# Filter spectra by one radix-2 step, issued one group late, with filter inputs on GpSimd's queue and other buffers at the end of the start-up

## The chip, the cores and the metric

The kernel runs on one core of a Trainium2 chip. The metric is the device time of one execution in microseconds. Three timed runs of the kernel before took 2672.59, 2676.36 and 2677.06 us; their median, 2676.36 us, stands for it.

## The reference

Two layers of a diffusion backbone work on 256 latent tokens of width 2048, with 256 context tokens ahead of them: layer 0 is a Mamba-2 group beside a latent attention group, layer 1 a Hyena long convolution, and a SwiGLU feed-forward layer follows each. Every sub-layer is normed and modulated by shift, scale and gate that come from the conditioning vectors. The parts that this case touches are the modulation and the filters of layer 1:

```python
mod = (c_act @ mod_w[i] + mod_b[i])[:, None, :]
sh1, sc1, g1, sh2, sc2, g2 = jnp.split(mod, 6, axis=-1)
n_lat = modulate(rms_norm(x, norm_mix_w[i]), sh1, sc1)
...
hid = jnp.sin(fr * (emb @ fw1 + fb1))
for j in range(HY_INNER):
    hid = jnp.sin(fr * (hid @ fw_mid[j] + fb_mid[j]))
...
for i, gate in enumerate((x1, x2)):
    h_two = jnp.einsum('lf,fkd->lkd', hid, fw_out[:, i]) * window[:, None, :]
    k = jnp.concatenate([h_two[:, 0], zeros, jnp.flip(h_two[1:, 1], axis=0)])   # 512 x 2048
    k = k / jnp.sum(jnp.abs(k), axis=0, keepdims=True)
    kf = jnp.fft.rfft(k, axis=0)
    y = gate * (irfft(rfft(y, n=512) * kf)[:256] + fbias[i] * y)
```

The filters depend on no token, so the kernel computes their spectra at its start, beside the first modulation.

## The kernel before, in words

Products in fp32 are made of three: each operand is split into a high part (`fp32r`, on ScalarE, L347) and the remainder (on VectorE, L348), and `mm3` (L375 to L382) multiplies high by high (L380), low by high (L381) and high by low (L382).

The start-up (`startup`, from L1347) runs four generators by turns. A small function, `turn`, always advances the one that has done the least against its entry in `START_RATE`; `START_AT` gives the filters one turn of handicap. A scheduler then sets the order on each engine, while each queue (SP's for loads, ScalarE's for the stores of spectra) keeps the order in which its transfers were issued.

- `filters` (L703 to L787): loads of the small net's inputs (L707 to L712), three layers of matmul (L722) and sine (`sin_layer`, L691 to L702), then eight groups of 512 channels: four channel blocks by two filters. A group loads its output weights `fwr` (256 KB, L742) and in every other group a window `win` (512 KB, L748) on SP's queue, and splits the weights. For two halves of the 256 positions and for the sum and the difference of the two directions it makes a product `pss`, multiplies it by the window (`sv`, L762), splits that (`sh`, `sl`), takes its absolute value (L766) and the larger of the two (`am`, L768). Then come the norm `psl` (8 products with a column of ones, which stand as 16 instructions, L774, and a reciprocal L776) and four spectra `psk`: each is two halves by three matmuls, 24 in all, copied by ScalarE into `ko` (L785; three buffers) and stored to `kscr` (256 KB each, L786, ScalarE's queue).
- `on_pe`: the first modulation of layer 0, on TensorE: 32 tiles of 1 MB of modulation weights (`mraw`, L1375, whole or as two halves in the buffers of the weight ring), matmuls `ps_mod` (L1378), a row (L1381), a transpose `ps_modT` (L1385) and the scaling of the tokens (L1398).
- `stats(0)` and `stats(1)`: the tokens x and the context `cin` are loaded (L309, L1410), squared (L492) and summed (L498) for the norms.

When the filters are through, their memory is given back and the normed tokens `act` are written as high and low parts (`halves`: L1446 on ScalarE, L1447 on VectorE), the rest of the modulation tiles is worked off, and `fetch` loads and splits the first three weight blocks `w_in` of layer 0, whose matmuls stand in L380 to L382 and, in their steady form, L813.

The other modulations (160 tiles of 1 MB, `mods` with the load L446) are worked off beside the projections of layer 0: `run` adds a share to `mod_debt` for each weight block and issues a tile whenever it has reached 1 (L426 to L429); VectorE reduces a tile by one operation (L453). At the output projection of layer 0, `mods_until(80)` forces what is still missing up to tile 80.

## Time and profile before

| what | value |
|---|---|
| three runs | 2672.59, 2676.36, 2677.06 us; median 2676.36 |
| profiled execution | 2675.05 us, its span 2673.2 us |
| mean granted TensorE clock of the span | 0.991 of full speed |
| instructions in the span | 39,653 |
| moved by DMA | 635.88 MB, mean 238 GB/s |

The span runs from the first to the last instruction of one execution, and 1.85 us of its time lie outside it. TensorE is called PE in the rows, its weight loads PEld, VectorE DVE, ScalarE ACT, GpSimd POOL and SyncE SP. `L380` is line 380 of the kernel. `out<-in` are the program's names of what an instruction writes and reads, `x24` is a count. Matmuls overlap each other, so the busy time of one (0.40 us) is longer than the distance of their starts.

### The profile page before, as it was taken

The page shows a single profiled execution, that of the slowest core. Times are in us where ns is not written, and L with a number is a line of the kernel's source. Part 1 is how long each engine was busy: PE and PEld are TensorE (multiplying, and loading weights), DVE is VectorE, ACT ScalarE, POOL GpSimd, SP SyncE. Part 2 cuts the span into 40 slices and gives each one's busy share as a digit, 9 for nine tenths or more (in the row PEclk, how much of TensorE's full clock was granted, in tenths as well). Part 3 has the DMA queues.
Part 4 walks back from the last instruction along what each step waited for, and adds up shares of the span by engine and source line. Part 5 has one row for each costly group of instructions (what it writes and reads, how often), then busy time and mean ns, then how long its engine had stood idle before and what let it go on. Part 6 is the DMA issues. An engine that isn't in the chain of part 4 may idle for free.

```text
span 2673.2 us, 39653 instructions
## 1 busy us (share of the span) xinstructions
PE 2604.5 (97%) x15288; PEld 2226.7 (83%) x15288; DVE 2068.4 (77%) x3138; ACT 1436.9 (54%) x2314; POOL 0.9 (0%) x10
## 2 busy tenths in 40 slices
PE   5989999999999999999999999999999999999998
PEld 2557778988998888888888888888988888888887
DVE  6458777868898987988879999998887656656656
ACT  4453665655654454544546755555644544544545
POOL 0000000000000000000000000000000000000000
PEclk8999999999999999999999999999999999999999
DMA  8876556647588987987987555456577655655543
GB/s 332 291 256 230 187 186 250 248 150 251 199 321 293 343 323 277 342 313 281 347 298 274 195 175 186 170 184 224 203 288 267 215 185 162 214 174 190 203 155 130
DMA packets 108861, 635.88 MB, mean 238 GB/s; under 512 B 11648, under 2 KB 20224, under 8 KB 48256
## 3 DMA queue, kind: packets, MB, share of 16 engines
q1 hardware_dynamic: 104064, 624.95, 65.3%
q10 hardware_dynamic: 4608, 8.39, 0.8%
q8 instruction: 121, 1.98, 0.3%
q14 instruction: 68, 0.56, 0.1%
HBM read 622.81 MB, written 10.49 MB: 237 GB/s over the span
## 4 chain that ended last, share of the span: by engine, by line
PE 90%; DVE 4%; DMA 3%; ACT 2%; issue 1%; SPq 0%; DVEq 0%; ACTq 0%
PE acc L569 41%; PE acc L570 22%; PE acc L813 6%; PE acc L572 3%; PE acc L380 2%; PE acc L382 2%; PE acc L381 2%; PE ps_mod L1378 1%; DMA kscr<-ko 1%; DVE wlo L348 1%; DMA raw<-in_w 1%; PE ps_c L380 1%; ACT whi L347 1%; PE ps_c L382 1%; PE ps_c L381 1%
## 5 line engine op out<-in xcount | busy, mean ns | idle before, releaser
L569 PE MATMUL acc<-act,whi 128*128 128x512 f32 x3525 | 1255.4, 396 | 2.5 <-ACT whi L347 2.5
L348 DVE TENSOR_TENSOR wlo<-raw,whi 128x1024 fp32r<-128x1024 f32 (+1 forms) x842 | 936.2, 1117 | 228.9 <-ACT whi L347 220.1
L347 ACT ACTIVATE whi<-raw 128x1024 fp32r<-128x1024 f32 (+1 forms) x842 | 813.4, 972 | 482.9 <-PE acc L569 243.0
L570 PE MATMUL acc<-act,wlo 128*128 128x256 f32 x3760 | 1020.8, 281 | 1.6 <-DVE wlo L348 1.3
L569 PEld LDWEIGHTS acc<-act,whi 128*128 128x128 f32 x3525 | 665.8, 189 | 149.0 <-ACT whi L347 3.3
L570 PEld LDWEIGHTS acc<-act,wlo 128*128 128x128 f32 x3760 | 709.0, 189 | 23.2 <-DVE wlo L348 2.9
L569 PE MATMUL acc<-hh,whi 128*128 128x512 f32 x1280 | 457.7, 395 | 0.0
L453 DVE SCALAR_TENSOR_TENSOR mraw<-mraw,cb 128x2048 f32<-128x2048 f32 x160 | 365.7, 2286 | 52.0 <-DMA mraw<-in_mod 51.7
L570 PE MATMUL acc<-hh,wlo 128*128 128x256 f32 x1408 | 377.1, 282 | 2.2 <-ACT hh L347 2.2
L569 PEld LDWEIGHTS acc<-hh,whi 128*128 128x128 f32 x1280 | 241.4, 189 | 51.0
L570 PEld LDWEIGHTS acc<-hh,wlo 128*128 128x128 f32 x1408 | 265.3, 189 | 14.9 <-ACT hh L347 2.5
L579 ACT ACTIVATE sum<-acc 128x256 f32<-128x256 f32 x160 | 61.4, 384 | 264.5 <-PE acc L572 264.4
L381 PE MATMUL acc<-act,whi 128*128 128x258 f32 (+1 forms) x560 | 160.0, 286 | 6.3 <-DVE act L1447 6.3
L380 PE MATMUL acc<-act,whi 128*128 128x258 f32 (+1 forms) x560 | 160.8, 288 | 5.2 <-ACT whi L347 4.9
L382 PE MATMUL acc<-act,wlo 128*128 128x258 f32 (+1 forms) x560 | 159.6, 285 | 0.8 <-DVE wlo L348 0.7
L582 DVE TENSOR_TENSOR sum<-sum,acc 128x256 f32<-128x256 f32 x203 | 84.8, 418 | 96.4 <-ACT sum L579 96.3
L813 PE MATMUL acc<-act,whi 128*128 128x512 f32 x480 | 157.5, 406 | 0.0
L591 ACT ACTIVATE res<-acc,mcol 128x256 f32<-128x256 f32 x144 | 68.1, 474 | 128.5 <-PE acc L572 125.5
L594 DVE SCALAR_TENSOR_TENSOR res<-acc,mcol,res 128x256 f32<-128x256 f32 x160 | 76.9, 481 | 66.2 <-ACT res L591 53.1
L381 PEld LDWEIGHTS acc<-act,whi 128*128 128x128 f32 x560 | 107.2, 192 | 7.4 <-DVE act L1447 6.9
L380 PEld LDWEIGHTS acc<-act,whi 128*128 128x128 f32 x560 | 107.3, 192 | 5.8 <-ACT whi L347 5.1
L382 PEld LDWEIGHTS acc<-act,wlo 128*128 128x128 f32 x560 | 107.4, 192 | 2.0 <-DVE wlo L348 1.9
(329 smaller groups left out, 2795.2 us busy)
## 6 DMA issues: line engine op xcount, KB each, us to landing
raw<-in_w SPq DMA_DIRECT2D x176, 1024.0 KB, 4.9
mraw<-in_mod SPq DMA_DIRECT2D x160, 1024.0 KB, 5.7
raw<-in_w SPq DMA_DIRECT2D x128, 704.0 KB, 4.3
raw<-in_hw_in SPq DMA_DIRECT2D x48, 1024.0 KB, 4.8
raw<-in_w_in SPq DMA_DIRECT2D x29, 1024.0 KB, 5.6
mraw<-in_modn SPq DMA_DIRECT2D x16, 1024.0 KB, 8.2
mraw<-in_modn SPq DMA_DIRECT2D x32, 512.0 KB, 7.3
raw<-in_w_o SPq DMA_DIRECT2D x16, 1024.0 KB, 4.9
```

Source lines behind the costliest of these rows:

```text
L347: nc.scalar.activation(hi, src, AF.Copy)
L348: nc.vector.tensor_tensor(lo, src, hi.bitcast(F32), ALU.subtract)
L380: t.matmul(out, lh, rh, start=first, stop=False)
L381: t.matmul(out, lh, rl, start=False, stop=False)
L382: t.matmul(out, ll, rh, start=False, stop=last)
L453: self.nc.vector.scalar_tensor_tensor(raw, raw, 1.0, self.cb, ALU.mult, ALU.mult, accum_out=self.mcol[:, j:j + 1])
L569: t.matmul(*high, start=kt == 0, stop=False, skip_group_check=True)
L570: t.matmul(ps[:, :S], wl, x[:, 0], start=False, stop=False, skip_group_check=True)
L572: t.matmul(*high, start=False, stop=True, skip_group_check=True)
L582: nc.vector.tensor_tensor(v, v, halves[0], ALU.add)
L594: nc.vector.scalar_tensor_tensor(v, halves[0], gate, v, ALU.mult, ALU.add)
L813: t.matmul(ps.rearrange("p (a b) -> p a b", a=2), w, self.act[:, j, :, kt, :S], start=kt == 0 and k == 0, stop=kt == n - 1 and k == 2)
```

## The change

- The length-512 transform of a filter is split by one radix-2 step: positions are stored with the even ones first and the odd ones behind (tables `embT` and `win`), each half is multiplied by the shorter table `dft_f` that the kernel already has (256 KB in place of `dft_k`'s 512 KB), and the two halves are added and subtracted. A group's 24 spectrum matmuls become 12; ScalarE copies the odd product (2 per group in place of 4 copies), VectorE adds and subtracts (4 per group), and the stores are 2 of 512 KB in place of 4 of 256 KB.
- These spectra stand in a generator of their own (`spectra`) that a group runs after the next group's products, one group late. The norm comes last in it; the two halves' maxima are added on VectorE first, so that it has 4 products (8 instructions) in place of 8 (16).
- The filter inputs `fwr` and `win` are loaded on GpSimd's queue; `win` and `sv` have two buffers.
- The first step of the filters is taken ahead of everything else, so its inputs stand first in SP's queue; `cols`, the tokens and `mats` follow. `START_RATE` changes, `START_AT` goes.
- After the filters' end the modulation tiles have a pool of their own, `mring` (3 x 1 MB, in memory given back by the filters), and the first weight blocks are loaded and split between the turns.
- `MOD_HOLD` lets `mod_debt` start at -3, so three tiles fewer are issued beside the projections of layer 0 (39 in place of 42), and they are forced at its output.

```diff
-START_RATE = (28, 38, 60, 40)
-START_AT = (1, 0, 0, 0)
+START_RATE = (38, 40, 60, 40)
+MOD_HOLD = 3
...
-        self.mod_debt = 0.0
+        self.mod_debt = -float(MOD_HOLD)
...
         nc.sync.dma_start(embT, a["embT"])
-        nc.sync.dma_start(self.mats, a["mats"])
         rawf = self.wraw.tile([P, KT * P], F32, tag="raw", name="raw_dftf")
-        nc.sync.dma_start(rawf[:, :1024], a["dft_k"].rearrange("p a b -> p (a b)"))
-        fh = pool.tile([P, 2, 512], F32R, name="fh0")
-        fl = pool.tile([P, 2, 512], F32R, name="fl0")
-        self.split(fh.rearrange("p a b -> p (a b)"), fl.rearrange("p a b -> p (a b)"), rawf[:, :1024])
+        nc.sync.dma_start(rawf[:, :512], a["dft_f"].rearrange("p a b -> p (a b)"))
+        fh = pool.tile([P, 2, 256], F32R, name="fh0")
+        fl = pool.tile([P, 2, 256], F32R, name="fl0")
+        yield
+        self.split(fh.rearrange("p a b -> p (a b)"), fl.rearrange("p a b -> p (a b)"), rawf[:, :512])
...
         yield
         wt = None
+        last = None
         for gi in range(8):
             g, i = gi // 2, gi % 2
             fwr = pool.tile([P, 512], F32, tag="fwr", name=self.nm("fwr"), bufs=2)
-            nc.sync.dma_start(fwr, a["fw"][i, g])
+            nc.gpsimd.dma_start(fwr, a["fw"][i, g])
             fwh = pool.tile([P, 512], F32R, tag="fwh", name=self.nm("fwh"), bufs=2)
             fwl = pool.tile([P, 512], F32R, tag="fwl", name=self.nm("fwl"), bufs=2)
             self.split(fwh, fwl, fwr)
             if i == 0:
-                wt = pool.tile([P, 2, 512], F32, tag="win", name=self.nm("win"), bufs=1)
-                nc.sync.dma_start(wt, a["win"][g])
+                wt = pool.tile([P, 2, 512], F32, tag="win", name=self.nm("win"), bufs=2)
+                nc.gpsimd.dma_start(wt, a["win"][g])
             s2 = []
-            am = []
-            for w, hx in ((0, hs), (1, hd)):
+            for w in range(2):
                 sh = pool.tile([P, 2, 512], F32R, tag=f"sh{w}", name=self.nm("sh"), bufs=2)
                 sl = pool.tile([P, 2, 512], F32R, tag=f"sl{w}", name=self.nm("sl"), bufs=2)
                 s2.append((sh, sl))
+            am = pool.tile([P, 512], F32, tag="am", name=self.nm("am"), bufs=2)
             for tt in range(2):
                 two = []
                 for w, hx in ((0, hs), (1, hd)):
                     ps = self.ps.tile([P, 512], F32, tag="ms", name=self.nm("pss"))
                     sl_ = slice(tt * P, (tt + 1) * P)
                     self.mm3(ps, (hx[:, 0, sl_], hx[:, 1, sl_]), (fwh, fwl), True, True)
-                    sv = pool.tile([P, 512], F32, tag=f"sv{w}", name=self.nm("sv"), bufs=1)
+                    sv = pool.tile([P, 512], F32, tag=f"sv{w}", name=self.nm("sv"), bufs=2)
                     nc.vector.tensor_tensor(sv, ps, wt[:, tt, :], ALU.mult)
                     self.split(s2[w][0][:, tt, :], s2[w][1][:, tt, :], sv)
                     two.append(sv)
+                amt = am if tt == 0 else pool.tile([P, 512], F32, tag="am1", name=self.nm("am1"), bufs=1)
                 for sv in two:
                     nc.scalar.activation(sv, sv, AF.Abs)
-                amt = pool.tile([P, 512], F32, tag="am", name=self.nm("am"), bufs=2)
                 nc.vector.tensor_tensor(amt, two[0], two[1], ALU.max)
-                am.append(amt)
+                if tt:
+                    nc.vector.tensor_tensor(am, am, amt, ALU.add)
                 yield
-            ps = self.ps.tile([P, 512], F32, tag="ms", name=self.nm("psl"))
-            for ct in range(4):
-                for tt in range(2):
-                    nc.tensor.matmul(ps[:, ct:ct + 1], am[tt][:, ct * P:(ct + 1) * P], self.mat("ones")[:, 0:1],
-                                     start=tt == 0, stop=tt == 1)
-            nc.vector.reciprocal(self.kinv[:, i * 16 + g * 4:i * 16 + g * 4 + 4], ps[:, 0:4])
-            for f, (c0, w) in enumerate(((0, 0), (128, 0), (256, 1), (384, 1))):
-                tag = ("ms", "acc")[f % 2]
-                ps = self.ps.tile([P, 512], F32, tag=tag, name=self.nm("psk"), bufs=3)
-                for tt in range(2):
-                    sl_ = slice(c0, c0 + P)
-                    self.mm3(ps, (fh[:, tt, sl_], fl[:, tt, sl_]), (s2[w][0][:, tt], s2[w][1][:, tt]),
-                             tt == 0, tt == 1)
-                ko = pool.tile([P, 512], F32, tag="ko", name=self.nm("ko"), bufs=3)
-                nc.scalar.activation(ko, ps, AF.Copy)
-                nc.scalar.dma_start(self.kscr[gi][:, f * 512:(f + 1) * 512], ko)
-            yield
+            if last:
+                yield from last
+            last = self.spectra(pool, fh, fl, gi, s2, am)
+        yield from last
+
+    def spectra(self, pool, fh, fl, gi, s2, am):
+
+        nc = self.nc
+        g, i = gi // 2, gi % 2
+        for w in range(2):
+            two = []
+            for tt in (1, 0):
+                ps = self.ps.tile([P, 512], F32, tag=("acc", "ms")[tt], name=self.nm("psk"), bufs=3)
+                r = slice(w * P, (w + 1) * P)
+                self.mm3(ps, (fh[:, tt, r], fl[:, tt, r]), (s2[w][0][:, tt], s2[w][1][:, tt]), True, True)
+                two.append(ps)
+            odd = pool.tile([P, 512], F32, tag="odd", name=self.nm("kodd"), bufs=1)
+            nc.scalar.activation(odd, two[0], AF.Copy)
+            ko = pool.tile([P, 2, 512], F32, tag="ko", name=self.nm("ko"), bufs=2)
+            for f, op in ((0, ALU.add), (1, ALU.subtract)):
+                nc.vector.tensor_tensor(ko[:, f], two[1], odd, op)
+            nc.scalar.dma_start(self.kscr[gi][:, w * 1024:(w + 1) * 1024], ko.rearrange("p a b -> p (a b)"))
+            if w == 0:
+                yield
+        ps = self.ps.tile([P, 512], F32, tag="ms", name=self.nm("psl"))
+        for ct in range(4):
+            nc.tensor.matmul(ps[:, ct:ct + 1], am[:, ct * P:(ct + 1) * P], self.mat("ones")[:, 0:1], start=True, stop=True)
+        nc.vector.reciprocal(self.kinv[:, i * 16 + g * 4:i * 16 + g * 4 + 4], ps[:, 0:4])
+        yield
...
-        nc.sync.dma_start(self.cols, a["cols"])
...
-            if q % 2 == 0:
-                raw = self.wraw.tile([P, 4, 512], F32, tag="raw", name=self.nm("mraw"))
+            if self.mring is not None or q % 2 == 0:
+                raw = (self.mring or self.wraw).tile([P, 4, 512], F32, tag="raw", name=self.nm("mraw"))
                 return [(raw, 0, 4)]
...
         todo = []
+        self.mring = None
         with self.pool(name="filt", bufs=1) as fp:
             gens = [self.filters(fp), on_pe(), stats(0), stats(1)]
-            done = list(START_AT)
+            done = [0] * 4
             live = [True] * 4
+            next(gens[0])
+            nc.sync.dma_start(self.cols, a["cols"])
+            next(gens[2])
+            nc.sync.dma_start(self.mats, a["mats"])
 
...
-        halves()
-        while any(live):
-            turn()
+        with self.pool(name="mring", bufs=3, side="right") as self.mring:
             halves()
-        self.fetch([(a["w_in"][i], KT) for i in (3, 4, 0)], -1, 3)
+            first = [(a["w_in"][i], KT) for i in (3, 4, 0)]
+            n = 0
+            while any(live):
+                turn()
+                halves()
+                n += 1
+                if n % 2 == 0 and self.loaded < 3:
+                    self.landed.append(self.load(*first[self.loaded]))
+                    self.loaded += 1
+                if n % 2 == 1 and n > 4 and self.landed:
+                    self.ready.append(self.split_w(*self.landed.pop(0)))
+                    self.halved += 1
+            self.fetch(first, -1, 3)
         nc.sync.dma_start(self.cb, a["cvec"])
         nc.scalar.activation(self.cb, self.cb, AF.Silu)
```

SP's queue at the program's start. Before, with the modulation tile `mraw`, the tokens `x` and the context `cin` ahead of the filter net's inputs:

```order
L1351 DMA cT<-in_cT 128x32
L1353 DMA pick<-in_pick 128x2
L1354 DMA cols<-in_cols 128x647
L1375 DMA mraw_104<-in_modn 128x2048
L309 DMA x_110<-in_xT 128x2048
L309 DMA x_112<-in_xT 128x2048
L1410 DMA cin_114<-in_ctxT 128x2048
L1410 DMA cin_115<-in_ctxT 128x2048
L1375 DMA mraw_144<-in_modn 128x1024
L1375 DMA mraw_145<-in_modn 128x1024
L707 DMA hidw<-in_hidw 128x384
L709 DMA embT<-in_embT 128x256
```

And with the change:

```order
L1357 DMA cT<-in_cT 128x32
L1359 DMA pick<-in_pick 128x2
L699 DMA hidw<-in_hidw 128x384
L701 DMA embT<-in_embT 128x256
L703 DMA raw_dftf<-in_dft_f 128x512
L1433 DMA cols<-in_cols 128x647
L301 DMA x_111<-in_xT 128x2048
L301 DMA x_113<-in_xT 128x2048
L1435 DMA mats<-in_mats 128x1408
L1380 DMA mraw_171<-in_modn 128x2048
L1415 DMA cin_190<-in_ctxT 128x2048
```

The net's inputs `hidw` and `embT` have moved from places eleven and twelve to three and four, and the column table `cols` has moved behind them.

TensorE at a group's spectra. Before, one group's spectra `psk` with the norm `psl` among them; the filter's high and low parts are `sh` and `sl`, the table's `fh` and `fl`:

```order
L380 MATMUL psk_523<-sh_453,fh_171 128x512
L381 MATMUL psk_523<-sl_454,fh_171 128x512
L382 MATMUL psk_523<-sh_453,fl_172 128x512
L380 MATMUL psk_523<-sh_453,fh_171 128x512
L381 MATMUL psk_523<-sl_454,fh_171 128x512
L382 MATMUL psk_523<-sh_453,fl_172 128x512
L380 MATMUL psk_533<-sh_453,fh_171 128x512
L381 MATMUL psk_533<-sl_454,fh_171 128x512
L382 MATMUL psk_533<-sh_453,fl_172 128x512
```

And with the change, at a late spectrum between another group's products:

```order
L372 MATMUL pss_646<-fwh_602,hd 128x512
L373 MATMUL pss_646<-fwl_603,hd 128x512
L374 MATMUL pss_646<-fwh_602,hd 128x512
L372 MATMUL psk_665<-sh_497,fh_108 128x512
L373 MATMUL psk_665<-sl_498,fh_108 128x512
L374 MATMUL psk_665<-sh_497,fl_109 128x512
L1383 MATMUL ps_mod_758<-mraw_759,c_96 32x512 x4
L1383 MATMUL ps_mod_758<-mraw_786,c_96 32x512
L372 MATMUL psk_687<-sh_499,fh_108 128x512
L373 MATMUL psk_687<-sl_500,fh_108 128x512
L374 MATMUL psk_687<-sh_499,fl_109 128x512
L791 MATMUL psl_701<-mats,am_501 128x1 x4
```

A spectrum product has three matmuls instead of six, the inputs `sh_497` and `sh_499` are those of the group ahead of `fwh_602`, and the norm stands behind the products.

SP's queue at the end of the start-up, with the change: the last modulation tiles (here `mraw_1299` to `mraw_1363`) stand behind the loads of weight blocks (`raw`, from `in_w_in`), which need buffers that splits give back:

```order
L1380 DMA mraw_1209<-in_modn 128x2048
L1380 DMA mraw_1235<-in_modn 128x1024
L1380 DMA mraw_1236<-in_modn 128x1024
L344 DMA raw_1311<-in_w_in 128x2048
L344 DMA raw_1339<-in_w_in 128x2048
L1475 DMA cb<-in_cvec 128x2048
L344 DMA raw_1361<-in_w_in 128x2048
L344 DMA raw_1482<-in_w_in 128x2048
L1380 DMA mraw_1299<-in_modn 128x2048
L1380 DMA mraw_1305<-in_modn 128x2048
L1380 DMA mraw_1333<-in_modn 128x2048
L1380 DMA mraw_1341<-in_modn 128x2048
```

In the order before, all modulation tiles of this stage stand ahead of the first load of a weight block.

## Rows read from the trace of the kernel before

**Rows 1.** The head of the page, and its line of engines.

```profile
span 2673.2 us, 39653 instructions
PE 2604.5 (97%) x15288; PEld 2226.7 (83%) x15288; DVE 2068.4 (77%) x3138; ACT 1436.9 (54%) x2314; POOL 0.9 (0%) x10
```

**Rows 2.** Busy time by stretches: us, each engine's busy time, clock, DMA share, GB/s.

```profile
0.00:42.20 42.20, 16.68 (x50) 3.00 (x50) 22.96 (x62) 17.15 (x41) 0.20 (x4) 0.84 0.96 376
42.20:182.00 139.80, 130.21 (x660) 79.71 (x660) 74.89 (x143) 68.46 (x115) 0.00 (x0) 0.99 0.81 280
182.00:210.40 28.40, 20.92 (x138) 17.36 (x137) 25.09 (x56) 19.70 (x43) 0.19 (x2) 0.88 0.48 163
210.40:2673.20 2462.80, 2436.73 (x14444) 2126.67 (x14443) 1945.43 (x2879) 1331.54 (x2116) 0.52 (x4) 1.00 0.65 234
```

**Rows 3.** The chain of waits up to the first filter matmul: start, us, what.

```profile
3.54 11.65 DMA cin<-in_ctxT
...
24.91 0.53 DVE sin L691
...
32.01 3.62 PE ps_mod L1378 x14
...
42.23 0.50 PE pss L380
```

**Rows 4.** The timeline of ScalarE in the tail: start, us, what.

```profile
196.69 1.69 ACT L1446 ACTIVATE act<-x,mcol 128x256 fp32r<-128x256 f32 x4
198.29 1.69 ACT L1446 ACTIVATE act<-cin,mctx 128x256 fp32r<-128x256 f32 x4
```

**Rows 5.** DMA from 0 to 182 us: queues with share; transfers with size and us to landing.

```profile
DMA packets 14986, 55.00 MB, mean 302 GB/s; under 512 B 1920, under 2 KB 2176, under 8 KB 12032
...
q1 hardware_dynamic: 10656, 47.02, 73.0%
q10 hardware_dynamic: 4320, 7.87, 11.3%
...
fwr<-in_fw SPq DMA_DIRECT2D x8, 256.0 KB, 9.1
...
cols<-in_cols SPq DMA_DIRECT2D x1, 323.5 KB, 3.5
hidw<-in_hidw SPq DMA_DIRECT2D x1, 192.0 KB, 15.8
```

**Rows 6.** The timeline of PE in one filter group.

```profile
56.53 0.40 PE L381 MATMUL psk<-sl,fh 128*128 128x512 f32 x1
56.77 0.39 PE L382 MATMUL psk<-sh,fl 128*128 128x512 f32 x1
57.00 0.40 PE L380 MATMUL psk<-sh,fh 128*128 128x512 f32 x1
...
58.64 1.71 PE L774 MATMUL psl<-mats,am 128*128 128x1 f32 x14
```

**Rows 7.** Groups by line, 42.2 to 182 us: busy us, mean ns | idle before, releasers.

```profile
L348 DVE TENSOR_TENSOR sl<-sv,sh 128x512 fp32r<-128x512 f32 x32 | 21.2, 687 | 16.8 <-ACT sh L347 16.2
L762 DVE TENSOR_TENSOR sv<-pss,win 128x512 f32<-128x512 f32 x32 | 21.2, 688 | 7.4 <-PE pss L382 6.7
...
L785 ACT ACTIVATE ko<-psk 128x512 f32<-128x512 f32 x31 | 18.1, 596 | 44.7 <-DMA kscr<-ko 21.9 <-PE psk L382 17.4 <-PE ps_mod L1378 3.8
...
L768 DVE TENSOR_TENSOR am<-sv,sv 128x512 f32<-128x512 f32 x16 | 11.0, 688 | 15.6 <-ACT sv L766 15.6
```

**Rows 8.** Groups by line, 0 to 182 us: the sums of squares.

```profile
L498 DVE TENSOR_TENSOR acc<-acc,sq 128x256 f32<-128x256 f32 x30 | 12.0, 420 | 1.5
```

**Rows 9.** Busy time of ten us in the filter stretch.

```profile
80.00:90.00 10.00, 9.93 (x45) 4.76 (x44) 5.53 (x9) 5.90 (x12) 0.00 (x0) 1.00 1.04 361
```

**Rows 10.** The page's groups: the reduction of a later modulation tile.

```profile
L453 DVE SCALAR_TENSOR_TENSOR mraw<-mraw,cb 128x2048 f32<-128x2048 f32 x160 | 365.7, 2286 | 52.0 <-DMA mraw<-in_mod 51.7
```

More of the change, by code (lines that the diff above doesn't have):

```diff
@@ L163, in _filter_tables @@
     emb = np.concatenate([t, np.cos(fw), -np.sin(fw)], axis=-1).astype(f32)
+    order = np.concatenate([np.arange(0, S, 2), np.arange(1, S, 2)])
     embT = np.zeros((P, S), f32)
-    embT[:HY_EMB] = emb.T
+    embT[:HY_EMB] = emb[order].T
     lo = math.log(1.5) / 1e-2
@@ L169, in _filter_tables @@
     win = np.exp((-t * deltas[None, :]).astype(f32)).astype(f32)
-    win = win.reshape(2, P, 4, 512).transpose(2, 1, 0, 3)
+    win = win[order].reshape(2, P, 4, 512).transpose(2, 1, 0, 3)
     return embT, np.ascontiguousarray(win)
@@ L220, in _prepare @@
     a["rope"] = _rope_tables()
-    a["dft_k"] = _dft_filter()
     a["dft_f"] = _dft_forward()
```

5 lines of the change are left out of this document (removed).

## The prediction

> **What bounds the kernel now.** I read the page's head first, then the busy time by stretches, then the chain of waits, then the groups by line inside one stretch, then the DMA queues. The head [rows 1] says that TensorE is busy for 97% of 2673.2 us. That average does not decide this case, because the diff touches the start and nothing else but a count. So the second view is the table by stretch [rows 2], cut at three events: the first filter matmul (42.2), the last spectrum matmul (182.0) and the first of the steady projection matmuls (210.4). From 210.4 on PE is busy for 2436.7 of 2462.8 us: there only less PE work would help, and the change removes none. The 210.4 us ahead of it are the place. They fall into three parts with different limits.
>
> Start, 0 to 42.2: PE works 16.7 us and waits. The chain [rows 3] runs through the context load (11.65 us to landing), then the sums of squares on VectorE, then the sine layers of the filter net, which begin at 24.91 and end in the first filter matmul at 42.23. Inside, 3.62 us of modulation matmuls stand ahead of a net matmul.
>
> Filter stretch, 42.2 to 182: eight filter groups in 139.8 us, 17.5 us each, PE busy 130.2, VectorE 74.9, DMA share 0.81 [rows 2].
>
> Tail, 182 to 210.4: the last modulation matmuls, the writing of the normed halves on ScalarE, the first weight splits [rows 4]; PE is busy 20.9 of 28.4 us.
>
> A measurement of this kernel can tell about 0.2%, 5 us, from no change. The profiled execution took 2675.05 us, 1.85 more than its span; the median of the three timed runs, 2676.36, is 1.3 us above it. The sum below is made against 2675.05.
>
> **Start.** The SP queue now begins with the small inputs of the filter net (16 to 324 KB) and has the modulation and context tiles behind them. In before, the net's weights were issued twelfth and landed 15.8 us after issue, while the column table, third in the queue, took 3.5 [rows 5]. With six small loads first, the net's input is there at about 8 us and the first sine operation at 9 to 10 (estimate from those two rows). From there the three layers took 42.23 - 24.91 = 17.3 us [rows 3]. I keep that: the order still mixes sums of squares in, but the modulation piece may go. First filter matmul at 27: **15 us gained**, between 10 (the layers wait for other work on VectorE, as they do now) and 18 (the layers alone).
>
> **Filter groups on PE.** The 24 products per group become 12. Back to back, such matmuls start 0.23 us apart [rows 6] (their 0.40 of busy time each overlap), so 12 x 0.23 = 2.8 us go per group. The norm's 16 one-column instructions become 8: 14 of them took 1.71 us [rows 6], 0.122 each, 1.0 us. Together 3.8 us, over eight groups 30 us, if PE alone set the pace: 139.8 - 30 = 110, T (the end of the filters) = 27 + 110 = 137.
>
> **Filter groups elsewhere.** ScalarE loses 32 copies and gains 16 at 0.596 us: 9.5 us less, on an engine that is not the bound. Its wait for spectrum stores was 21.9 of the 44.7 us ahead of those copies [rows 7]; with two buffers of 512 KB, filled one group after their spectra's inputs, part of that goes. VectorE gains four adds per group out of PSUM (32 in all) and one add of sums (8): 40 x 0.688 [rows 7] = 27.5 us, and some 24 of the 30 sums of squares, 0.42 us each [rows 8], which all ran before 42.2 and will partly run here: 10 us. That makes 74.9 + 27.5 + 10 = 112 us of work for 110 us of PE time: no cover left. (The price of an add with an operand in PSUM is that of the window product, 0.688.) The transfers: 55.0 MB moved by 182 us [rows 5], six tiles of 1 MB now come after the end of the filters and two weight tiles earlier, so about 50 MB. Some 10 MB of them move in the first 27 us at the start's 376 GB/s [rows 2]; 39.8 are left. At the stretch's present 280 GB/s [rows 2] they take 142 us (T = 169), at the 361 GB/s of the ten us in which the DMA engines were full [rows 9], 110 us (T = 137). So PE, VectorE and the transfers all ask for about 110 us and none for less, and three equal demands never overlap fully. Between 137 and 169 I take the middle, **T = 153** (126 us, 15.8 per group, 316 GB/s): the store waits and the long wait at a group's end go, which speaks against 169; VectorE fed from ScalarE by turns (15.6 us of wait ahead of the maxima, 16.8 ahead of the low halves [rows 7]) speaks against 137. From 182 - 15 that is **14 us gained** (0 to 30, or 2 lost).
>
> Twelve filter loads move from SP's to GpSimd's queue. They no longer stand behind modulation tiles whose buffers are taken; behind them only a few fills are queued. I cost them at nothing; their cover is one group, 15.8 us, since the inputs have two buffers. For the whole of trn2's queues the Trainium skill, "DMA: Bandwidth & Descriptors", section "Rules for kernel authors", says that spreading transfers over issuing engines gives no bandwidth, only issue time. By that rule the gain here is only the freed place in the queue; the trace agrees so far that SP's and ACT's queues together make the share in [rows 5].
>
> **Tail.** The last six modulation tiles have buffers of their own, but in memory that the filters held, so they start at T and stand behind weight loads that wait for splits. Six MB at 361 GB/s take 17 us, so the last is there at T + 20; then its matmuls, the transposes, and the writing of four k-tiles per stream, 1.7 us each on ScalarE [rows 4]: steady matmuls at T + 27.5, against T + 28.4 now. PE meanwhile takes the 12 k-tiles that are ready. **1 us gained**, less 2 for a lower granted clock after a longer idle time (0.84 and 0.88 in the two idle stretches, 1.00 later [rows 2]).
>
> **Later.** Three later modulation tiles fewer are worked off beside the layer-0 projections and are forced at its output, 3 x 2.286 us of VectorE [rows 10] and 3 MB. PE is saturated around there; I take **1 us lost** (0 to 7).
>
> Sum: 15 + 14 + 1 - 2 - 1 = 27. **2675 - 27 = 2648 us.** All at its best, 18 + 30 + 1 - 3 = 46 with the same deductions: 2629; T = 169 gives 2664.
>
> **Rivals.** *VectorE sets the groups' pace.* For it: 112 us of work, and its present waits for ScalarE, 32.4 us [rows 7], come from a chain of four operations by turns that the change leaves as it is. If three quarters stay, 112 + 24 = 136 us, T = 163 to 164, gain 16 to 17: about 2658. Against it: the late spectra give it work that waits for nobody.
>
> *The transfers set the pace.* For it: 302 GB/s was the mean from 0 to 182 [rows 5]; 50 MB at that rate end at 166, gain 14: about 2661. Against it: full-rate stretches exist [rows 9], and the present gaps come from taken buffers. The skill's rule on queues above speaks for this rival.
>
> *Slower: GpSimd's loads land late.* The trace has no DMA on that queue. The nearest rows are the same loads on SP's (9.1 us) and the slowest small one (15.8) [rows 5]. The cover is 15.8 us; each us beyond it delays each of the six groups after the first two. The gain is gone at 15.8 + 27/6 = 20.3 us to landing, slower by over 0.2% from 21.2; at 25 it would be 2648 + 6 x 9.2 = 2703. The Trainium skill has a mechanism for it: "SBUF — State Buffer", section "Who interferes with whom", says that a VectorE copy or tensor_scalar in a two-port mode locks GpSimd out while it writes descriptors. In this trace such operations stand in the sine layers (0.3 us each), while the stretch's VectorE work is two-input operations [rows 7], so by that rule the lock-out is short. No row shows the queue at work.
>
> *The change doesn't take its place.* The order shows the late spectra, the norm last and the twelve loads on GpSimd's queue, so this is left only as: the tail gives it all back, within 0.2% of 2675.
>
> **How the numbers follow.** Forecast (2630 to 2655) 0.56; VectorE 0.19; transfers 0.17; late loads 0.04; given back 0.04. The range of eight in ten takes the forecast's case but its very best, and the two milder rivals: **2632 to 2664**. Faster by over 0.2%: 0.56 + 0.19 + 0.17 = 0.92; within: 0.04; slower: 0.04.
>
> **What would show it.** First filter matmul at about 27 us, filters' end at about 153, steady projection matmuls at about 180, and from there to the end the same 2463 us. Twelve spectrum matmuls per group at 0.23 us, VectorE busy over 80% in the stretch, DMA share near 0.9. Wrong if the first filter matmul stays behind 32 (the sine chain waits for something else), if PE's idle time in the groups ends with a filter input's landing (late loads), or if the stretch keeps its 17.5 us per group. If the time after the steady start grows by over 5 us, the forced modulation tiles are mis-sized.

## The result and the profile after

The changed kernel takes 2646.61 us (median of five runs, 2645.54 to 2648.84). The kernel before took 2676.36 us beside it. The ratio is 0.989, with a 95% interval of 0.9878 to 0.9901: faster by 29.75 us, where 2648 had been forecast (27 us, against the 2675.05 of the profiled execution). The profiled execution took 2648.55 us, its span is 2646.7, which is 26.5 less than before.

The head of the page after, for [rows 1]:

```profile
span 2646.7 us, 39320 instructions
PE 2572.2 (97%) x15128; PEld 2200.9 (83%) x15128; DVE 2088.8 (79%) x3178; ACT 1428.2 (54%) x2298; POOL 7.4 (0%) x22
```

Busy time by stretches, cut at the same three events as [rows 2]: the first filter matmul, the end of the last spectrum matmul, the steady projection matmuls.

```profile
0.00:26.70 26.70, 5.27 (x14) 1.26 (x14) 14.57 (x39) 7.97 (x18) 3.53 (x10) 1.00 0.92 365
26.70:148.60 121.90, 107.23 (x508) 56.90 (x508) 100.66 (x203) 68.81 (x122) 3.21 (x6) 0.94 0.85 322
148.60:190.30 41.70, 26.32 (x165) 18.08 (x166) 22.96 (x54) 18.40 (x41) 0.19 (x2) 0.71 0.64 237
190.30:2646.70 2456.40, 2433.38 (x14443) 2124.68 (x14441) 1950.63 (x2884) 1333.07 (x2119) 0.52 (x4) 1.00 0.65 235
```

Set beside [rows 2], the four stretches give: start 42.2 to 26.7 (15.5 gained), groups 139.8 to 121.9 (17.9 gained), tail 28.4 to 41.7 (13.3 lost), the rest 2462.8 to 2456.4 (6.4 gained). The sum is 26.5. The forecast had 15, 14, -1 and -1. Two of the four terms were far off, in opposite directions. A total that agrees says nothing of the parts here, and the experiments are about the parts.

To follow a gain through the program I read from the trace when the same instruction starts in each kernel. The columns: the first product `pss`, the last spectrum matmul `psk`, the first `ps_dup` (early in layer 0's projections), the first `ps_s` (layer 0's attention, ahead of its output projection), the first `hh` matmul (layer 0's feed-forward, behind it), the last `ps_c` (layer 1's convolution), the span. All in us.

| kernel | pss | psk | ps_dup | ps_s | hh | ps_c | span |
|---|---|---|---|---|---|---|---|
| before | 42.2 | 181.7 | 222.6 | 534.4 | 839.8 | 1820.2 | 2673.2 |
| after | 26.7 | 148.2 | 202.0 | 512.2 | 824.4 | 1803.0 | 2646.7 |
| e1 no hold | 26.6 | 148.0 | 204.4 | 515.3 | 820.5 | 1799.3 | 2651.6 |
| e2 filters on SP | 32.6 | 148.3 | 196.3 | 508.0 | 820.8 | 1796.3 | 2639.5 |
| e3 three spectra buffers | 27.2 | 146.7 | 196.0 | 507.7 | 820.2 | 1796.2 | 2640.0 |
| e4 less on VectorE | 27.5 | 142.9 | 192.7 | 504.5 | 817.4 | 1794.2 | 2637.9 |
| e5 not late | 28.4 | 156.4 | 207.8 | 519.5 | 834.5 | 1810.2 | 2654.0 |
| e6 no ring | 26.7 | 147.8 | 192.3 | 504.1 | 818.2 | 1793.7 | 2637.3 |
| e7 radix-2 alone | 41.0 | 181.7 | 227.6 | 539.4 | 845.5 | 1825.0 | 2674.4 |
| e8 order alone | 33.6 | 175.7 | 230.5 | 542.3 | 847.5 | 1826.4 | 2678.0 |
| e9 long transform, late | 28.8 | 152.6 | 204.0 | 514.2 | 828.8 | 1806.3 | 2650.1 |
| e10 one buffer each | 25.9 | 161.9 | 212.2 | 522.4 | 836.9 | 1812.5 | 2656.2 |
| e11 no ring, three buffers | 26.9 | 147.7 | 192.2 | 504.0 | 818.4 | 1794.0 | 2637.5 |
| e12 one product buffer | 26.9 | 154.5 | 204.6 | 514.8 | 829.7 | 1805.3 | 2649.6 |

The lead of the changed kernel over the kernel before, column by column, is 15.5, 33.5, 20.6, 22.2, 15.4, 17.2 and 26.5. It is made in the first two stretches. 13 us of it go in the tail, 7 more between the attention and the feed-forward of layer 0, and 9 come back behind layer 1's convolution, in code that the diff does not touch. From `ps_c` to the end of the span the ten kernels with the hold take 843.2 to 844.3 us, and the four without it (before, e1, e7, e8) 849.4 to 853.0.

The transfers up to 150 us, for [rows 5]:

```profile
DMA packets 11011, 49.51 MB, mean 330 GB/s; under 512 B 1526, under 2 KB 1782, under 8 KB 8182
...
q1 hardware_dynamic: 7915, 38.40, 67.0%
q10 hardware_dynamic: 1872, 6.82, 11.1%
q0 software_dynamic: 1216, 4.20, 8.1%
...
fwr<-in_fw POOLq DMA_DIRECT2D x8, 256.0 KB, 5.6
win<-in_win POOLq DMA_DIRECT2D x4, 512.0 KB, 6.2
...
hidw<-in_hidw SPq DMA_DIRECT2D x1, 192.0 KB, 3.3
```

GpSimd's queue shows as a row of its own (q0). Its filter loads land in 5.6 us, where SP's took 9.1. The net's weights land in 3.3 us instead of 15.8.

Groups by line in the filter stretch, for [rows 7]:

```profile
L755 DVE TENSOR_TENSOR sv<-pss,win 128x512 f32<-128x512 f32 x32 | 21.5, 686 | 14.2 <-PE pss L374 14.1
L340 DVE TENSOR_TENSOR sl<-sv,sh 128x512 fp32r<-128x512 f32 x32 | 20.9, 686 | 0.0
...
L785 DVE TENSOR_TENSOR ko<-psk,kodd 128x512 f32<-128x512 f32 x28 | 18.3, 683 | 0.0
...
L761 DVE TENSOR_TENSOR am<-sv,sv 128x512 f32<-128x512 f32 x16 | 11.0, 688 | 0.6 <-ACT sv L760 0.6
```

VectorE's waits for ScalarE, 16.8 ahead of the low parts and 15.6 ahead of the maxima in [rows 7], are down to 0.0 and 0.6: there is now other work to do at those points. What it still waits for is the product from TensorE (14.1). Its longest wait before was another one, for the norm, ahead of the reciprocal (us in total, times, the longest); before, and with the change:

```profile
DVE kinv L776 <- PE psl L774: 17.4, 7, 4.2
```

```profile
DVE kinv L792 <- PE psl L791: 3.0, 1, 3.0
```

The stretch is shorter by 17.9 us although VectorE has 25.8 us more of work in it (74.9 to 100.7): its idle time fell from 64.9 to 21.2 us.

### The profile page after: what moved, and what is told of

It is laid out like the page before. It is cut to its first block, busy times and chain, and to the rows that moved or that the text cites. A ratio compares the mean times of both kernels' runs of the same rounds, so it can differ in the third digit from the quotient of the medians.

```text
span 2646.7 us, 39320 instructions
## 1 busy us (share of the span) xinstructions
PE 2572.2 (97%) x15128; PEld 2200.9 (83%) x15128; DVE 2088.8 (79%) x3178; ACT 1428.2 (54%) x2298; POOL 7.4 (0%) x22
## 4 chain that ended last, share of the span: by engine, by line
PE 92%; DVE 4%; ACT 1%; issue 1%; DMA 1%; SPq 0%; DVEq 0%; ACTq 0%
PE acc L561 41%; PE acc L562 23%; PE acc L819 7%; PE acc L564 3%; PE acc L372 3%; PE acc L373 3%; PE acc L374 3%; PE ps_mod L1383 1%; DVE wlo L340 1%; PE ps_c L372 1%; PE ps_c L374 1%; PE ps_c L373 1%; DVE mraw L445 1%; PE ps_y L1070 0%; PE ps_o L1201 0%
```

## The experiments

Each was run in three rounds against the kernel before. Times are medians, and behind each ratio stands its interval. "Filters' end" is the column `psk` above; where `pss` differs too, a part of the difference is the start's (against the changed kernel 5.9 us later in e2, 1.7 in e5, 2.0 in e9, 0.8 in e4, 0.8 earlier in e10).

The medians of the kernel before beside these runs lie between 2672.1 and 2676.9 us, and each interval reaches 3 to 6 us to either side. Among the variants of the changed kernel only e1, e5 and e11 have intervals clear of its own (0.9878 to 0.9901). For the others, what is said of a few us rests on the columns above, of one trace each.

### e1: without the hold

```diff
-MOD_HOLD = 3
+MOD_HOLD = 0
```

> The changed kernel with MOD_HOLD = 0: three modulation tiles go back beside the projections of layer 0. Theory A (the 6 to 7 us that the changed kernel loses around layer 0's output projection are the forced tiles): the lead over the kernel before stays at 22 us through that projection instead of falling from 22 to 15, and if the two later gains (4 us near 1395 us, 10 us near 1945 us) do not hang on the count, the total is about 2640 us. Theory B (those later gains come from the other places of the tiles in the weight ring, that is from the same count): the loss and the gains both go, 2653 to 2657 us.

Measured: 2653.87 us, ratio 0.9926 (0.9902 to 0.995). Both theories hold, each for its half. Through layer 0's output the lead over before stays (19.1 at `ps_s`, 19.3 at `hh`), where the changed kernel falls from 22.2 to 15.4. Busy time around the output projection, the changed kernel first:

```profile
598.00:618.00 20.00, 15.48 (x68) 12.04 (x68) 13.15 (x27) 13.50 (x24) 0.13 (x1) 0.85 0.73 259
```

and e1:

```profile
598.00:618.00 20.00, 19.34 (x105) 15.70 (x104) 12.68 (x29) 15.37 (x29) 0.13 (x1) 1.00 0.63 230
```

With the hold TensorE is idle for 4.5 of 20 us, without it for 0.7, and its granted clock falls to 0.85. So the three tiles more that are forced here cost 6.8 us. In exchange the changed kernel is 3.1 us ahead of e1 at `ps_s` (22.2 against 19.1). 2.4 of these are there at `ps_dup` already: without the hold the first of the later tiles is loaded inside the tail, at 143.60 us, and the last six tiles of the first modulation follow from 153.71 instead of 146.74. The larger return is late. The changed kernel gains 9.3 us on before from `ps_c` to the end, and e1 only 0.7. The place is layer 1's feed-forward; the rows are, in order, of before, of the changed kernel and of e1:

```profile
1940.00:1960.00 20.00, 15.07 (x105) 14.49 (x104) 15.21 (x24) 8.77 (x15) 0.00 (x0) 0.83 0.72 254
```

```profile
1920.00:1940.00 20.00, 20.00 (x155) 19.31 (x154) 19.84 (x31) 8.86 (x15) 0.00 (x0) 1.00 0.74 276
```

```profile
1920.00:1940.00 20.00, 18.15 (x135) 17.63 (x134) 17.12 (x28) 10.94 (x18) 0.00 (x0) 0.91 0.72 267
```

Before and e1 have a hole here, the changed kernel has none. In the kernel before it is one wait of TensorE for a weight split, 4.9 us long:

```profile
PE acc L380 <- ACT whi L347: 4.9, 1, 4.9
```

Followed matmul by matmul, the lead of the changed kernel rises from 20.1 to 27.3 us across this hole; the rest of the 9.3 is a smaller pair of such waits near 1840 us, worth 2.9, less 0.8 given back at the end. The count of held tiles moves the later tiles to other places among the weight blocks of SP's queue, down to the last layer, and one of these orders leaves out the wait. That it hangs on the count is shown. Why this order avoids the wait was not traced further, and nobody should expect it of a hold in another kernel.

### e2: filter inputs on SP's queue again

```diff
-            nc.gpsimd.dma_start(fwr, a["fw"][i, g])
+            nc.sync.dma_start(fwr, a["fw"][i, g])
...
-                nc.gpsimd.dma_start(wt, a["win"][g])
+                nc.sync.dma_start(wt, a["win"][g])
```

> The changed kernel with fwr and win loaded on SP's queue again. Theory A (the queue is worth its free place only, the inputs have a group of cover): first filter matmul within 1 us, filters' end within 3 us of 148.6, time within 3 us of 2646.6. Rival (they then wait behind modulation tiles whose buffers are taken): filters' end at 155 to 165, time 2652 to 2662.

Measured: 2642.09 us, ratio 0.9884 (0.9863 to 0.9905), 4.5 us under the changed kernel's median, which neither theory had. The first product comes 5.9 us later: its weights `fwr` land at 25.6 us instead of 4.4, behind the tokens, the context and modulation tiles, and ScalarE splits them at 32.0, behind squares of the norms. The filters still end at the same time: the groups take 116.1 us instead of 121.9, and VectorE has 97.2 us of work in them instead of 100.7, having done more of its other work by then. So the early start that GpSimd's queue buys is worth nothing at the filters' end here. The 6 us that e2 gains in the tail come from another order of ScalarE's instructions, below.

### e3: three buffers of spectra

```diff
-            ko = pool.tile([P, 2, 512], F32, tag="ko", name=self.nm("ko"), bufs=2)
+            ko = pool.tile([P, 2, 512], F32, tag="ko", name=self.nm("ko"), bufs=3)
```

(and, for room, `embT` in the buffers tagged `hid`, and one buffer for `row`.)

> The changed kernel with three buffers of spectra for two (room for the third comes from the table embT, which shares a buffer, and from one row buffer less). Theory A (the last stores wait for each other's buffers, and ScalarE's writing of the normed tokens stands behind the last of them): the tokens are written from about 151 instead of 157.6 us, steady projection matmuls start some 5 us earlier, time about 2641. Rival (the last six modulation tiles set the tail, whose loads are as late as before): the writing starts earlier, but the time stays within 2 us of 2646.6.

Measured: 2642.66 us, ratio 0.9888 (0.9866 to 0.991); `ps_dup` at 196.0 instead of 202.0. Theory A holds. The tail of the changed kernel in its chain of waits:

```profile
147.75 7.98 DMA kscr<-ko
155.86 1.30 DVE ko L785 x2
157.18 0.33 ACTq L786
157.63 9.68 ACT act L1456 x24
167.31 0.49 ACT row L1386
167.84 1.87 PE ps_modT L1390 x8
169.71 1.86 PE ps_mod L1383 x8
171.57 0.51 PE acc L372
172.09 0.21 PE acc L373
...
175.41 0.12 PE acc L374
...
190.30 11.88 PE acc L819 x51
```

The last pair of adds waits for a store to give its buffer back (7.98 us from its issue to its landing; VectorE is idle for 4.65 of them), the last store's issue waits for the adds, and the token writes (9.68 us) stand behind that issue on ScalarE. Why the store came so late is in ScalarE's timeline:

```profile
147.69 1.06 ACT L339 ACTIVATE whi<-raw 128x1024 fp32r<-128x1024 f32 x1 [5.35 <-PE ps_mod L1383]
147.75 0.33 ACTq L786 DMA_DIRECT2D kscr<-ko  x1
```

Its spectra were ready at 143.7, but on ScalarE the store's issue stands behind a weight split, and the split waited 5.35 us for modulation matmuls to free its buffer. The split stands there because the change lays the first weight blocks between the turns. With three buffers the same store is about as late (issued at 146.33), but nobody waits for its buffer, as the chain of e3 shows:

```profile
146.27 1.07 ACT whi L339
...
150.82 1.30 DVE ko L785 x2
152.14 0.33 ACTq L786
152.59 9.68 ACT act L1456 x24
```

In e2 the scheduler happened to put that store ahead of the split (issued at 142.16), with the same effect.

### e4: subtractions off VectorE

```diff
-                nc.vector.tensor_tensor(ko[:, f], two[1], odd, op)
+                if f:
+                    nc.scalar.activation(ko[:, f], two[1], AF.Copy)
+                else:
+                    nc.vector.tensor_tensor(ko[:, f], two[1], odd, op)
```

> The changed kernel with the 16 subtractions of the odd product left out: ScalarE copies the even product in their place, so half of the spectra are not those of the reference. VectorE has 16 x 0.65 = 10 us less in the filter stretch, ScalarE 10 us more. Theory A (VectorE sets the pace of the groups now: 100.7 of 121.9 us busy): filters' end 6 to 10 us earlier, at 139 to 143. Rival 1 (the transfers set it, at 322 GB/s): end within 3 us of 148.6. Rival 2 (TensorE, 107 of 121.9 us): the same as rival 1, and TensorE's idle share does not change.

Measured: 2639.48 us, ratio 0.9871 (0.9846 to 0.9897). The filters end 5.3 us earlier, for 10 us of work taken from VectorE: just under theory A's range, and outside both rivals'. So about half of the 10 us shows: VectorE's work is part of what sets the pace, not all of it. The edit also shortens the chain, since a copy of the even product waits for no odd one; how much of the 5.3 us is due to that was not separated. The row of the stretch:

```profile
27.50:143.30 115.80, 106.66 (x508) 58.68 (x508) 94.20 (x190) 75.05 (x138) 3.22 (x6) 0.92 0.90 339
```

With VectorE lighter, TensorE is at 106.7 of 115.8 us and the transfers at 0.90. These are the next candidates; that they are bounds is not shown by a share alone (e7).

### e5: spectra not late

```diff
-            if last:
-                yield from last
-            last = self.spectra(pool, fh, fl, gi, s2, am)
-        yield from last
+            yield from self.spectra(pool, fh, fl, gi, s2, am)
```

> The changed kernel with each group's spectra and norm issued behind its own products, not one group late. Theory A (the lateness gives TensorE and VectorE work that waits for nobody; without it each group again waits for the chain product, window, high part, low part, spectrum): filters' end 10 to 16 us later than 148.6, time 2654 to 2662. Rival (the stretch is set by the sum of VectorE's and the transfers' work, whatever its order): end within 4 us, time within 4 us of 2646.6.

Measured: 2656.82 us, ratio 0.9936 (0.9921 to 0.9952). Filters' end 8.2 us later, which is less than theory A's 10 to 16 and more than the rival's 4; time within theory A's range. Lateness is worth 8 us at the filters' end, 6.5 of them inside the groups (128.4 us instead of 121.9). Without it VectorE waits ahead of its adds for ScalarE's copy of the odd product, where the changed kernel waits 0.0:

```profile
DVE ko L782 <- ACT kodd L779: 9.9, 6, 4.4
```

### e6: no buffers of their own for the last modulation tiles

```diff
-        with self.pool(name="mring", bufs=3, side="right") as self.mring:
+        if True:
```

> The changed kernel without the pool of its own for the last modulation tiles: they share the weight buffers again, while the first weight blocks are loaded between the turns as in the change. Theory A (own buffers let the tiles load beside the weight blocks): the tail from the filters' end to the steady matmuls gets 4 to 10 us longer, time 2650 to 2657. Rival (the tail waits for the last spectrum stores and the token writes; the pool lies in memory that the filters give back, so it costs as much as it brings): the tail is the same or shorter, time 2641 to 2648.

Measured: 2639.32 us, ratio 0.9866 (0.9851 to 0.9882). The rival's direction holds, by more than it said (2641 to 2648): without the pool it is 7.3 us faster. In the changed kernel the six loads into the pool, whose memory the filters give back only at their end, stretch over 25 us of SP's timeline. The second of them is issued at 159.86, right behind the landing of the last spectrum store at 159.79, so the pool too waits for the late stores of e3:

```profile
146.74 25.22 SPq L1380 DMA_DIRECT2D mraw<-in_modn  x6
```

In e6 the last tiles share the weight buffers; they are issued at 125.6, 140.8 and about 150 to 152 us, and the last modulation matmuls start at 167.0 instead of 183.0. The chain of e6:

```profile
151.05 11.69 DMA mraw<-in_modn
162.78 1.92 PE ps_mod L1383 x4
164.70 0.51 PE acc L372
...
179.67 12.82 PE acc L819 x55
```

A modulation tile is what comes last now (11.69 us from issue to landing), and the steady matmuls start at 179.7 instead of 190.3.

### e7: the radix-2 step alone, in the kernel before

```diff
-            for f, (c0, w) in enumerate(((0, 0), (128, 0), (256, 1), (384, 1))):
-                tag = ("ms", "acc")[f % 2]
...
+            for w in range(2):
+                pq = []
+                for tt in (1, 0):
+                    ps = self.ps.tile([P, 512], F32, tag=("acc", "ms")[tt], name=self.nm("psk"), bufs=3)
+                    r = slice(w * P, (w + 1) * P)
+                    self.mm3(ps, (fh[:, tt, r], fl[:, tt, r]), (s2[w][0][:, tt], s2[w][1][:, tt]), True, True)
+                    pq.append(ps)
```

(then copy, two adds and store as in the change, and the tables in even and odd order.)

> The kernel before with the radix-2 spectra alone (12 matmuls, one copy, two adds and one store per half; norm first, spectra behind their own group, loads, rates and buffers as before). Theory A (TensorE set the pace of the groups in the kernel before): the stretch 42 to 182 us loses 2.8 us per group, 15 to 22 us in all, time 2655 to 2661. Rival (the chain of a group sets it, so that fewer matmuls only make TensorE wait): the stretch loses under 8 us, time 2668 or more.

Measured: 2673.7 us, ratio 0.9988 (0.9975 to 1.0001). The rival's numbers hold: the filters end at the same 181.7 us with 96 matmuls fewer. The row of its filter stretch:

```profile
41.00:182.10 141.10, 127.97 (x570) 73.49 (x570) 90.61 (x170) 59.52 (x99) 0.00 (x0) 0.83 0.75 276
```

TensorE's busy time went down by only 2.2 us from [rows 2], although 96 spectrum matmuls at 0.23 us are 22 us of it. Its granted clock fell from 0.99 to 0.83, and its matmuls on the filters now start 0.33 us apart in the median instead of 0.23. So the busy share hardly moved (91% after 93%) while 22 us of work at the full clock went: such a share does not tell what the removal of matmuls will give. Two things stay open. The run also puts four adds per group on VectorE (90.6 us of work after 74.9), so it shows what the radix-2 step brings as a whole, not what fewer matmuls alone would. And whether the group's chain or the lower clock holds the stretch at 141 us is not separated.

### e8: the order of the loads alone, in the kernel before

```diff
-START_RATE = (28, 38, 60, 40)
+START_RATE = (38, 40, 60, 40)
...
-            done = list(START_AT)
+            done = [0] * 4
             live = [True] * 4
+            next(gens[0])
+            nc.sync.dma_start(self.cols, a["cols"])
+            next(gens[2])
+            nc.sync.dma_start(self.mats, a["mats"])
```

> The kernel before with the small inputs first in SP's queue, the column table and the tokens behind them and the new rates, nothing else. Theory A (the early start moves everything): first filter matmul at 28 to 33 instead of 42.2 us, filters' end 10 to 14 us earlier, time 2662 to 2667. Rival (what the filters gain at the start they lose, because the modulation tiles come later and TensorE's work is the same): filters' end within 4 us of 182, time 2671 to 2677.

Measured: 2682.66 us, ratio 1.0029 (1.0018 to 1.004): slower than either theory had it. The first product comes 8.6 us earlier and the filters' end 6.0 (between the two theories), but the modulation is pushed behind the filters: its last matmul starts at 195.4 instead of 185.0, and `ps_dup` comes 7.9 us later. The early start is worth something only if the rest of the start-up keeps up.

### e9: the long transform, late

```diff
-        nc.sync.dma_start(rawf[:, :512], a["dft_f"].rearrange("p a b -> p (a b)"))
...
+        nc.sync.dma_start(rawf[:, :1024], a["dft_k"].rearrange("p a b -> p (a b)"))
...
+            for f in range(2):
...
+                r = slice((2 * w + f) * P, (2 * w + f + 1) * P)
+                for tt in range(2):
+                    self.mm3(ps, (fh[:, tt, r], fl[:, tt, r]), (s2[w][0][:, tt], s2[w][1][:, tt]), tt == 0, tt == 1)
+                nc.scalar.activation(ko[:, f], ps, AF.Copy)
```

> The changed kernel with the long transform again: 24 spectrum matmuls per group, four copies on ScalarE, no adds, stores and lateness as in the change (the table embT shares a buffer to make room). Per group TensorE has 2.8 us more, VectorE 2.4 us less. Theory A (once spectra are late, TensorE's work sets the pace, which is why the shorter transform alone brought nothing in the kernel before): filters' end 10 to 20 us later than 148.2, time 2656 to 2667. Rival (VectorE sets the pace in either form, and the lateness is all that counts): end within 4 us of 148.2 or earlier, time 2640 to 2651.

Measured: 2650.82 us, ratio 0.99 (0.9875 to 0.9924). Filters' end 4.4 us later, far less than theory A's 10 to 20 and just over the rival's bound; time in the rival's range. Its stretch:

```profile
28.80:153.00 124.20, 119.57 (x590) 72.14 (x591) 85.71 (x174) 75.97 (x138) 3.22 (x6) 0.97 0.85 309
```

TensorE is busy for 119.6 of 124.2 us here at a clock of 0.97; that it sets the pace is likely, but a share is all there is for it. 2.0 of the 4.4 us are there at the first product already, so the groups themselves are only 2.3 us longer. So the step named first in the change's own words, the shorter transform with its adds, is worth some 4 us at most at the filters' end, where the groups overlap (e7: nothing where they do not).

### e10 and e12: one buffer

```diff
-                wt = pool.tile([P, 2, 512], F32, tag="win", name=self.nm("win"), bufs=2)
+                wt = pool.tile([P, 2, 512], F32, tag="win", name=self.nm("win"), bufs=1)
...
-                    sv = pool.tile([P, 512], F32, tag=f"sv{w}", name=self.nm("sv"), bufs=2)
+                    sv = pool.tile([P, 512], F32, tag=f"sv{w}", name=self.nm("sv"), bufs=1)
```

(e10 has both edits, e12 the second alone.)

> The changed kernel with one buffer each for the window and the windowed products, as in the kernel before. Theory A (the second buffers let the next half's products be written while the absolute values of the last half are still read): filters' end 4 to 10 us later, time 2650 to 2657. Rival (the lateness alone fills the gaps): end within 3 us, time within 4 us of 2646.6.

Measured, e10: 2656.94 us, ratio 0.9921 (0.9899 to 0.9943). Filters' end 13.7 us later, more than theory A's 10. From its chain of waits:

```profile
87.46 10.08 DMA win<-in_win
```

With one buffer the window's load cannot be issued before the last product with the old window, and the chain then runs through its 10.08 us from issue to landing. VectorE is idle for 6.7 us in two such waits (us in total, times, the longest):

```profile
DVE sv L755 <- DMA win<-in_win: 6.7, 2, 6.2
```

Its waits for ScalarE are back in part: 6.1 us ahead of the low parts and 2.8 ahead of the maxima.

> The changed kernel with one buffer for the windowed products, but two for the window: it splits the 14 us that the filters' end came later with one buffer of each. Theory A (the window: its load cannot start before the last product with the old one, and lands some 6 us later, three times): end within 4 us of 148.2, time 2644 to 2651. Rival (the products: the next half's are held until the absolute values and the maximum have read the last half's): end at 156 to 162, time 2652 to 2658.

Measured, e12: 2651.55 us, ratio 0.9919 (0.9897 to 0.9941). The end is 6.3 us later, between the two theories: the products' buffer is worth 6 us. The other 7 are put down to the window's buffer by difference; it was not taken away alone.

### e11: both edits of the tail

> The changed kernel with both edits of the tail that ran faster alone: no pool of its own for the last modulation tiles, and three buffers of spectra for two. If the two gains are separate (7 us and 4 us): about 2635. If both take away the same wait (the token writes behind the last stores): 2638 to 2640.

Measured: 2638.48 us, ratio 0.9854 (0.9834 to 0.9875). The second case holds: it stands with e6 (2639.32), not under it. In e6 the tail no longer waits for the stores but for a modulation tile, so a third buffer has nothing left to take away. e6 is the change minus one line and beats both kernels.

## Why the prediction came out right, and where its steps were not

**Start: right.** Forecast 27 for the first product, measured 26.7; the net's first sine operation starts at 10.47 us, forecast 9 to 10. What it waited for was not the net's inputs, which had landed by 6.88, but the column table `cols`, which the change moved behind them:

```profile
10.47 0.53 DVE L683 TENSOR_SCALAR sin<-psh,cols 64x256 f32<-64x256 f32 x1 [0.70 <-DMA cols<-in_cols]
```

(The prediction calls the net's weights the twelfth load of SP's queue before; `hidw` stood eleventh and `embT` twelfth.)

**Filter groups: size nearly right (14 forecast, 17.9 measured), cause wrong.** The step that failed is "Filter groups on PE": it priced the change by TensorE's matmuls, 30 us "if PE alone set the pace", and took half of that for the waits. The runs show in its place that the radix-2 step brings 0 at the filters' end of the kernel before (e7), and 4.4 in the changed kernel (e9). What shortened the groups is, for the larger part, what the prediction named in the change and gave no price: the second buffers of window and product (13.7 us, e10; 6.3 of them the product's, e12) and the lateness (8.2, e5). The worths are not additive: each is what its absence costs in the finished kernel, and neither was put alone into the kernel before. The prediction had read the waits of VectorE for ScalarE in [rows 7] and counted them to rivals. They fell from 31.8 us to 0.6, and came back in part without the buffers (8.9 in e10, 8.5 in e12); the wait for the norm fell from 17.4 us to 3.0, and the prediction has for it at most its "long wait at a group's end", without a number. A busy share of TensorE (130.2 of 139.8) was taken for a bound; e7 has nearly the same share with 96 matmuls fewer.

**VectorE: priced by rows, and a true rival.** The prediction counted 112 us of work in the stretch at the mean time of one instruction. The rows of VectorE in it do add up to about 112 us, 9.4 of them sums of squares (10 forecast). The busy time is 100.7 because rows overlap: a mean is no rate, as the timeline of VectorE in the changed kernel shows:

```profile
139.39 0.69 DVE L785 TENSOR_TENSOR ko<-psk,kodd 128x512 f32<-128x512 f32 x1
139.99 0.68 DVE L763 TENSOR_TENSOR am<-am,am 128x512 f32<-128x512 f32 x1
140.59 0.69 DVE L785 TENSOR_TENSOR ko<-psk,kodd 128x512 f32<-128x512 f32 x1
```

Back to back they start 0.60 apart, not 0.69. The prediction had made this very correction for matmuls [rows 6] and not for VectorE. In e4 the filters end 5.3 us earlier for 10 us of VectorE's work less.

**GpSimd's queue: costed at nothing, and that holds for the filters' end (e2).** The late-loads rival fell: the loads land in 5.6 us against a cover of 15.2 (121.9 / 8). The Trainium skill, "DMA: Bandwidth & Descriptors", section "Rules for kernel authors", has the rule that spreading over issuing engines gives no bandwidth. The trace agrees: up to 148 us the mean is 329 GB/s with three queues and 335 with two (e2). The Trainium skill, "SBUF — State Buffer", section "Who interferes with whom", says that a VectorE operation can lock GpSimd out while GpSimd writes descriptors. No run here shows such a delay: GpSimd's issues took 0.53 to 0.68 us each in every run that has them.

**Tail: wrong by 12 us.** The forecast was 27.5 us and 2 more for the lower clock, against 28.4 before; measured 41.7. The step that failed is "steady matmuls at T + 27.5". It let the token writes run beside the loads of the last tiles and asked nothing of ScalarE's order. There a weight split, a store, a pair of adds and the writes stand one behind the other (e3), and the pool that was to help holds its tiles back (e6). The lower clock was there as forecast: 0.71, matmuls 0.21 us apart instead of 0.12 until 175 us. But the waits were the larger part: in e6 the steady matmuls start 10.6 us earlier.

**Later: -1 forecast, +6.4 measured.** The forced tiles cost 6.8 us at layer 0's output, the end of the stated 0 to 7 and not the 1 that was taken. The gain of 9 us late in layer 1 was in no case: it came with the tiles' new places, which e1 takes away again. It also hid the sign that the prediction had set for mis-sized tiles, a longer time after the steady start.

So the total came out right by luck: 12 us too little in the tail's price and 6 in the forced tiles' were made up by 4 in the groups and 13 that came later, 9 of them through another order of tiles and weight blocks.

## What to carry to other kernels

Take the part of a change that is easiest to count, and ask what in the stretch waits for what before you price it: here the step that halves the spectrum matmuls was worth nothing by itself, and 4 us beside two second buffers and a delay of one group, which were worth more. A busy share near 1 of an engine whose instructions overlap is a reason to look at its releasers, not proof of a bound. And where work is moved into gaps, look at what is queued behind it on an in-order engine: one split between two turns held back a store, its buffer, and the whole tail.

## What the runs showed of the hardware that was not expected

A stretch with fewer matmuls ran at a lower granted clock: 0.83 in e7 against 0.99 before, in the same 140 us, so that TensorE's busy time hardly fell (130.2 to 128.0 us). A lower clock also shows around layer 0's output, where it is 0.85 in the changed kernel against 1.00 in e1: TensorE is idle for 4.5 us there, and the lead falls by 6.8. In the hole of the kernel before near 1945 us TensorE lacks 4.9 us of busy time at a granted clock of 0.83, and the lead of the changed kernel rises by 7.2 us across it. So both waits on TensorE's path cost more than their length.
